# A fused encoder layer on one core: three instead of six low parts made by accumulating DMAs in the opening, and the first unit's products and one sum of h in another order

## The chip, the cores and the metric

The program runs on one core of a Trainium2 chip. The metric is the device time of one execution in microseconds (us); less is better. Before the change the median of three runs is 1087.13 us (1085.92 to 1087.98).

## What is computed

One encoder layer on a sequence of 512 tokens of width 1024, all in float32. A conditioning vector `c` gives nine modulation vectors (shift, scale and gate of three sublayers), then come a SwiGLU, two token mixers in parallel, and a second SwiGLU:

```
mod = silu(c) @ w_mod + b_mod                      # 1024 -> 9 x 1024
sh1, sc1, g1, sh2, sc2, g2, sh3, sc3, g3 = split(mod, 9)
h = rmsnorm(x, norm_ffn1) * (1 + sc1) + sh1
x = x + 0.5 * g1 * swiglu(h, w_ffn1_in, w_ffn1_out)      # inner width 2816
...                                                       # two attention mixers, gated
h = rmsnorm(x, norm_ffn2) * (1 + sc3) + sh3
x = x + 0.5 * g3 * swiglu(h, w_ffn2_in, w_ffn2_out)
```

Only the beginning matters here: the norm of `x`, `sc1` and `sh1`, `h`, and the first products with `w_ffn1_in`.

## The kernel before, in words

**High and low parts.** Every matrix product is made of three: each operand is split into a high part (rounded to a shorter format by a copy on ACT) and a low part (the rest), and high*high, high*low and low*high are summed in PSUM. A low part is made in one of two ways. Either DVE subtracts the high part from the raw tile (L607 in the opening, L786 in units, L170 in `split_from`), or ACT writes minus the raw tile, rounded, into the place of the low part (L600), and an accumulating DMA issued by POOL adds the matrix from HBM once more (L601).

**The opening** (`first_chunk`, L644 to L683) runs over k = 0 to 7, slices of 128 of the 1024 channels. For each k three transfers of 512 KB are queued on SP: the columns of `w_mod` for sc1 (called SC1 k here), the tile `w1s[k]` (raw k) and the columns for sh1 (SH1 k). DVE reduces each `w_mod` tile with silu(c) (L269), then L335 makes `x * scale * norm`, ACT adds the shift and rounds (L336: h high), and DVE makes the low part of h (L338). PE multiplies with L637: eight products of 512 columns with h high, eight with h low, and eight with the weights' low part, which from k = 1 on are put off (`rest1`) and come one or two chunks later. So PE needs 24 products for k = 0, 16 for k = 1 and 2, 24 for k = 3 to 6 and 40 for k = 7. The order on DVE is written out by hand: L335 of k, L269 for SC1 k+1, L338 of k, L269 for SH1 k+1, L607 of k+1 where there is one, and L335 of k+1.

`BY_DMA` (L115) lists the k whose low part is made by L600 and L601. The others have L607.

**The first unit** (`First`, L765 on) begins when the last L637 ends. A unit multiplies in Strassen's manner with seven products (24 matmuls of 256 columns each) instead of eight; their weights are the quarters a11, a12, a22 and the sums s1 = a21+a22, s2 = s1+a11, s3 = a11+a21, s4 = s2+a12, and their other operands the quarters of h and the sums n1, n2, t3, t4 (`h1_sum`, L750). s1, s3 and s4 come from accumulating DMAs of POOL (L778), s2 from DVE (L794). High parts of weights: L782 on ACT; low: L786 on DVE. Sums of h: L562 or L564 on DVE, L169 on ACT, L170 on DVE. Products of a11, s2, s3 and a22 share one PSUM bank (x), s1 and s4 another (v), a12 has a third (w). After a11, s1 and s2, ACT copies the bank out (L838), after s3 DVE adds it (L844), and the next product into that bank has to wait for it.

**The order of work.** All instructions of this stage stand in an order that the program computes from a list of steps with times (`steps1`) and tasks with due times (`tasks1`): a task is written down after the first step whose time is not smaller. `First.first` is the order of the products of the first unit, `times` in `First.tasks` holds the due times of the splits, and a tuple at L1009 those of the sums of h. The unit of `times` is one product, 2.72. Each engine then executes its instructions strictly in the order written.

Of the kernel before, what the change touches and what calls it, by code (L numbers as in the profile page):

```python
# [111 lines left out]

LAST = 2

BY_DMA = (1, 2, 3, 5, 6, 7)  # L115

TO_MIX = (4, 2, 2, 2, 4, 2, 1)
TO_FFN2 = (3, 1, 2, 2, 3, 2, 1)
# [6 lines left out]
def layer(ctx: ExitStack, tc: tile.TileContext, a: dict):  # L125
# [34 lines left out]
    def f(ap):  # L160
        return ap.bitcast(F32)
# [432 lines left out]
    def first_split(k):  # L594
# [3 lines left out]
        S.copy(hi, raw)  # L598
        if k in BY_DMA:
            S.activation(lo, raw, AF.Identity, scale=-1.0)  # L600
# [3 lines left out]
    def first_low(k):  # L604
        raw, hi, lo = w1[k][2:]
        if k not in BY_DMA:
            V.tensor_tensor(lo, raw, f(hi), ALU.subtract)  # L607
# [4 lines left out]
    n1 = Norm()  # L612
# [110 lines left out]
    n2 = Norm()  # L723
    act_h, act_l, act_t = [None] * NPAIR, [None] * NPAIR, {}

    def new_act(p):
        part = [r for r in ROUNDS if p in r][0]
        i = (p - part.start) // 4
        if (part.start, i) not in act_t:
            act_t[part.start, i] = b8(), b8()  # L730
            for q in range(part.start + 4 * i, min(part.start + 4 * i + 4, part.stop)):
                act_h[q], act_l[q] = (t[:, q - part.start - 4 * i, :] for t in act_t[part.start, i])
        return act_t[part.start, i], (p - part.start) % 4
# [16 lines left out]
    def h1_sum(t):  # L750

        p, q = SUMS[t]
        out = h1_at[q if t in ("t3", "t4") else p]
        if t == "t3":
            h1_op[t] = [u[:, :, HALVES[1]] for u in h1_tiles]
        else:
            o = b8()
            h1_op[t] = [o[:, :, r] for r in HALVES]
        for k in (slice(0, 2), slice(2, 4)):
            sub(out[:, k, :], h1_at[p][:, k, :], h1_at[q][:, k, :], t in NEGATED)  # L760
        for k in (slice(0, 2), slice(2, 4)):
            split_from(*(u[:, k, :] for u in h1_op[t]), out[:, k, :])
        h1_at[t] = out

    class First(Unit):  # L765

        order = ("a11", "s1", "s2", "a12", "s3", "s4", "a22")
        first = ("a11", "a12", "s1", "s2", "s3", "s4", "a22")

        def load(self, q):  # L770
            t = u4(F32).rearrange("p a b -> p (a b)") if q == "s1" else sbuf("raw", [P, 1024], F32, RAW)
# [26 lines left out]
        def tasks(self):  # L798
            early = self is units1[0]
            yield -6.7 if early else -13.0, lambda: self.load("s1")  # L800
            yield -5.3 if early else -11.0, lambda: self.add("s1", "s1", "a22")
            yield -6.5 if early else -9.5, lambda: self.load("a11")
            second = self is units1[1]
            yield -0.3 if early else -2.4 if second else -5.9, self.second
            yield -5.6 if early else -5.0, lambda: self.load("a12")
            yield -1.0, lambda: self.load("a22")
            times = dict(s1=-7, a11=-3, s2=-2, a12=-1, s3=2, s4=3, a22=3)
            if early:
                times.update(s1=-1.2, a11=-2.5, s2=-0.02, a12=-1.6, s4=3.05, a22=3.1)
            if second:  # L810
                times.update(s1=-3.5, s2=-1.5, a11=-4.2)
            for q, at in times.items():
                yield at, lambda q=q: self.high(q)
                yield at + (0.4 if early else 1.0), lambda q=q: self.low(q)
# [181 lines left out]
    def task1(at, do):  # L996
        heapq.heappush(tasks1, (at, task1.n, do))
        task1.n += 1
# [7 lines left out]
        task1(19.0 + 2.0 * q, lambda q=q: finish_high(q))  # L1006
        task1(21.0 + 2.0 * q, lambda q=q: finish_low(q))
    new_act(0)
    for t, at in (("n1", -16.0), ("n2", -5.0), ("t3", 2.6), ("t4", 11.0)):  # L1009
        task1(at, lambda t=t: h1_sum(t))  # L1010

    def multiply1(u, q, t0, last):
# [703 lines left out]
    with tc.manual_schedule(engines=BOUND):  # L1716
# [6 lines left out]
        at = TO_FFN2  # L1723
# [177 lines left out]
```

## Time and profile before

| | before |
|---|---|
| median of the runs | 1087.13 us (1085.92 to 1087.98) |
| the profiled execution, its own time | 1087.35 us |
| its span, first to last instruction | 1085.5 us |
| PE, DVE, ACT, POOL busy | 97%, 74%, 53%, 13% of the span |
| mean granted clock of PE | 0.997 |
| opening, from the first L637 to the first product of the first unit | 16.67 to 68.42 us |

The profile is one execution on the chip. A row of the timeline gives the start in us, the duration in us, engine, line, operation, tiles (written <- read), shapes and count, and in brackets how long the engine was idle before and who ended that. In the table by windows the columns are the length of the stretch, busy time and count of PE, PE's weight loads, DVE, ACT and POOL, the granted PE clock, the busy share of the DMA engines, and GB/s. The granted clock is told as a share of full speed. A duration on DVE or ACT can overlap the next one's start by some hundredths; the distance from start to start is what an instruction costs in a row of them.

### The profile page before, as it was taken

How to read it: one execution, taken by the hardware profiler on the slowest of the kernel's cores; microseconds unless marked ns; L12 is line 12 of the kernel's file. 1: busy time of each engine (PE TensorE's matmuls, PEld its weight loads, DVE VectorE, ACT ScalarE, POOL GpSimd, SP SyncE). 2: the span in 40 equal slices, each digit the busy share in tenths (PEclk: the TensorE clock that was granted, in tenths of full speed). 3: DMA queues.
4: the chain of work that ended last, by engine and by line, in shares of the span. 5: the costliest groups of instructions: out<-in, count | busy, mean ns of one | idle time of the engine just before them, and what ended most of it. 6: DMA issues, size and time to landing. Idle time of an engine off the chain costs nothing.

```text
span 1085.5 us, 18432 instructions
## 1 busy us (share of the span) xinstructions
PE 1057.8 (97%) x7228; PEld 952.8 (88%) x7228; DVE 800.8 (74%) x1446; ACT 574.0 (53%) x937; POOL 145.9 (13%) x165
## 2 busy tenths in 40 slices
PE   8799999999999999999999999999999999999998
PEld 6689889989998988866788877989999999999997
DVE  7768777687967845657853777995878776877877
ACT  6555335424653443666645556534765645654553
POOL 1110010001001100521002300001021111211210
PEclk9999999999999999999999999999999999999999
DMA  9995986788666394864358821885397999999974
GB/s 345 341 227 144 313 239 163 191 281 228 166 207 220 111 316 152 182 146 97 98 173 203 224 88 57 331 286 141 78 208 173 225 225 238 197 228 217 215 149 121
DMA packets 65193, 215.64 MB, mean 199 GB/s; under 512 B 7762, under 2 KB 9938, under 8 KB 65107
## 3 DMA queue, kind: packets, MB, share of 16 engines
q1 hardware_dynamic: 44496, 145.73, 38.9%
q0 software_dynamic: 18160, 64.50, 32.4%
q10 hardware_dynamic: 2450, 4.25, 1.0%
q8 instruction: 56, 0.92, 0.3%
q14 instruction: 31, 0.25, 0.1%
HBM read 205.53 MB, written 8.92 MB: 198 GB/s over the span
## 4 chain that ended last, share of the span: by engine, by line
PE 67%; issue 15%; DMA 8%; DVE 6%; POOL 2%; ACT 2%; ACTq 0%; SPq 0%; POOLq 0%; DVEq 0%
PE sc L164 6%; PE sc L166 6%; PE sc L165 5%; PE acc L434 3%; PE acc L435 3%; PE acc L436 3%; PE sc L436 3%; PE sc L434 3%; PE sc L435 3%; PE acc L164 3%; PE acc L165 3%; PE acc L166 3%; DMA u<-w2i 2%; PE acc L1132 2%; PE acc L1133 2%
## 5 line engine op out<-in xcount | busy, mean ns | idle before, releaser
L434 PE MATMUL acc<-b,high 128*128 128x256 f32 x614 | 170.9, 278 | 1.7 <-ACT f L838 0.7
L435 PE MATMUL acc<-b,high 128*128 128x256 f32 x614 | 170.5, 278 | 0.4 <-DVE b L170 0.3
L436 PE MATMUL acc<-b,low 128*128 128x256 f32 x614 | 170.3, 277 | 0.1
L169 ACT CAST high<-raw 128x1024 fp32r<-128x1024 f32 (+1 forms) x96 | 98.8, 1032 | 116.5 <-PE sc L1134 19.0
L170 DVE TENSOR_TENSOR low<-raw,high 128x1024 fp32r<-128x1024 f32 (+1 forms) x96 | 114.8, 1200 | 56.4 <-ACT high L169 56.2
L434 PE MATMUL sc<-b,high 128*128 128x256 f32 x550 | 152.3, 277 | 2.6 <-ACT f L502 2.6
L436 PE MATMUL sc<-b,low 128*128 128x256 f32 x550 | 152.3, 277 | 0.1
L435 PE MATMUL sc<-b,high 128*128 128x256 f32 x550 | 152.1, 277 | 0.0
L434 PEld LDWEIGHTS acc<-b,high 128*128 128x128 f32 x614 | 115.7, 188 | 2.8 <-ACT f L838 0.9
L435 PEld LDWEIGHTS acc<-b,high 128*128 128x128 f32 x614 | 115.8, 189 | 0.9 <-DVE b L170 0.5
L436 PEld LDWEIGHTS acc<-b,low 128*128 128x128 f32 x614 | 115.8, 189 | 0.3 <-DVE low L170 0.3
L434 PEld LDWEIGHTS sc<-b,high 128*128 128x128 f32 x550 | 103.3, 188 | 3.0 <-ACT f L502 3.0
L436 PEld LDWEIGHTS sc<-b,low 128*128 128x128 f32 x550 | 103.3, 188 | 0.5 <-DVE low L786 0.3
L435 PEld LDWEIGHTS sc<-b,high 128*128 128x128 f32 x550 | 103.3, 188 | 0.0
L165 PE MATMUL sc<-b,high 128*128 128x512 f32 (+1 forms) x272 | 99.1, 364 | 0.2 <-DVE b L170 0.2
L166 PE MATMUL sc<-b,low 128*128 128x512 f32 (+1 forms) x272 | 99.0, 364 | 0.3 <-DVE low L880 0.3
L164 PE MATMUL sc<-b,high 128*128 128x512 f32 (+1 forms) x272 | 99.0, 365 | 0.0
L164 PE MATMUL acc<-b,high 128*128 128x512 f32 (+1 forms) x200 | 74.6, 373 | 1.2 <-ACT b L169 0.6
L169 ACT CAST high<-u 128x1024 fp32r<-128x1024 f32 (+1 forms) x51 | 52.2, 1026 | 40.2 <-PE sc L435 9.3
L269 DVE CUSTOM_DVE_ANT_0 u<-u,ka,begin 128x1024 f32<-128x1024 f32 x48 | 62.6, 1310 | 13.9 <-DMA u<-w_mod 13.8
L170 DVE TENSOR_TENSOR low<-u,high 128x1024 fp32r<-128x1024 f32 (+1 forms) x51 | 60.7, 1191 | 15.0 <-ACT high L169 14.4
L165 PE MATMUL acc<-b,high 128*128 128x512 f32 (+1 forms) x200 | 71.7, 359 | 0.0
(382 smaller groups left out, 2711.4 us busy)
## 6 DMA issues: line engine op xcount, KB each, us to landing
u<-w_mod SPq DMA_DIRECT2D x66, 512.0 KB, 6.6
raw<-w2i SPq DMA_DIRECT2D x31, 512.0 KB, 5.1
u<-w2i POOLq DMA_DIRECT2D x31, 512.0 KB, 6.3
raw<-w1u SPq DMA_DIRECT2D x27, 512.0 KB, 5.3
u<-w1u POOLq DMA_DIRECT2D x18, 512.0 KB, 7.7
raw<-w1o SPq DMA_DIRECT2D x16, 512.0 KB, 4.4
raw<-w_gate SPq DMA_DIRECT2D x16, 512.0 KB, 4.1
low<-w_gate POOLq DMA_DIRECT2D x13, 512.0 KB, 7.4
```

The source lines that it names most:

```text
L164: PE.matmul(out, wh, xh, start=first, stop=False)
L165: PE.matmul(out, wh, xl, start=False, stop=False)
L166: PE.matmul(out, wl, xh, start=False, stop=last)
L169: S.copy(hi, src)
L170: V.tensor_tensor(lo, src, f(hi), ALU.subtract)
L269: summed = V.tensor_tensor_reduce(out=w, in0=w, in1=cact, scale=by, scalar=b, op0=ALU.mult, op1=ALU.add, accum_out=t,)
L434: PE.matmul(out, wh[:, s], xh, start=first and j == 0, stop=False, skip_group_check=True)
L435: PE.matmul(out, wh[:, s], xl, start=False, stop=False, skip_group_check=True)
L436: PE.matmul(out, wl[:, s], xh, start=False, stop=last and j == 1, skip_group_check=True)
L1132: PE.matmul(out[t][:, 0:n], hh[k][:, ht], wh[:, o : o + n], start=k == 0, stop=False)
L1133: PE.matmul(out[t][:, 0:n], hh[k][:, ht], wl[:, o : o + n], start=False, stop=False)
```

## The change

The low parts of k = 2, 3 and 6 are made by L607 on DVE, not by L600 and L601. In the first unit s2 is multiplied before s1. Of the due times, s4's split moves from 3.05 to 2.9 products, and the sum t4 from 11.0 to 8.0; s3 keeps its 2.

```diff
-BY_DMA = (1, 2, 3, 5, 6, 7)
+BY_DMA = (1, 5, 7)
...
         order = ("a11", "s1", "s2", "a12", "s3", "s4", "a22")
-        first = ("a11", "a12", "s1", "s2", "s3", "s4", "a22")
+        first = ("a11", "a12", "s2", "s1", "s3", "s4", "a22")
...
             if early:
-                times.update(s1=-1.2, a11=-2.5, s2=-0.02, a12=-1.6, s4=3.05, a22=3.1)
+                times.update(s1=-1.2, a11=-2.5, s2=-0.02, a12=-1.6, s3=2, s4=2.9, a22=3.1)
...
-    for t, at in (("n1", -16.0), ("n2", -5.0), ("t3", 2.6), ("t4", 11.0)):
+    for t, at in (("n1", -16.0), ("n2", -5.0), ("t3", 2.6), ("t4", 8.0)):
```

**DVE in the opening**, a piece of the difference between the two programs, around k = 2 and k = 3. raw_152 is raw 2 and raw_232 raw 3; x_80 and x_81 are the slices of x for k = 2 and 3.

```order
 L269 ISA u_29_154,mod_96<-u_29_154,ka_112,par 128x1024
 L269 ISA mod_96 128x1
+L607 TENSOR_TENSOR low<-raw_152,high 128x1024
 L335 SCALAR_TENSOR_TENSOR b_16_117<-x_80,mod_97,f_53_227 128x512
 L269 ISA u_55_230,mod_97<-u_55_230,ka_112,begin,par 128x1024
...
 L269 ISA u_57_234,mod_96<-u_57_234,ka_112,par 128x1024
 L269 ISA mod_96 128x1
+L607 TENSOR_TENSOR low<-raw_232,high 128x1024
 L335 SCALAR_TENSOR_TENSOR b_16_117<-x_81,mod_97,f_53_227 128x512
```

The subtract stands ahead of L335, which begins the making of h for the same k. A third one is added in the same place for k = 6; on ACT the three L600, and on POOL's queue three of the six L601, are gone. SP's queue has the same transfers in the same order.

**DVE in the first unit**, before. raw_442 is the tile of s3, u_70_440 that of s4, raw_573 that of a22, raw_534 that of the second unit's a11, acc_538 bank x, and the pair L562 and L170 is t4.

```order
L841 TENSOR_TENSOR f_83_587<-f_83_587,tp_589 128x512
L786 TENSOR_TENSOR low<-raw_442,high 128x1024
L786 TENSOR_TENSOR low<-u_70_440,high 128x1024
L786 TENSOR_TENSOR low<-raw_573,high 128x1024
L786 TENSOR_TENSOR low<-raw_534,high 128x1024
L844 TENSOR_TENSOR f_87_655<-f_87_655,acc_538 128x512
L562 SCALAR_TENSOR_TENSOR b_17_118<-b_16_117,b_17_118 128x2x256 x2
L170 TENSOR_TENSOR b_89_740<-b_17_118,b_89_740 128x2x256 x2
```

The same place with the change (the numbers in the names have moved: s3 is raw_439, s4 u_70_437, a22 raw_570, the second unit's a11 raw_531, bank x acc_535).

```order
L841 TENSOR_TENSOR f_83_584<-f_83_584,tp_586 128x512
L786 TENSOR_TENSOR low<-raw_439,high 128x1024
L562 SCALAR_TENSOR_TENSOR b_17_118<-b_16_117,b_17_118 128x2x256 x2
L170 TENSOR_TENSOR b_88_681<-b_17_118,b_88_681 128x2x256 x2
L786 TENSOR_TENSOR low<-u_70_437,high 128x1024
L786 TENSOR_TENSOR low<-raw_570,high 128x1024
L786 TENSOR_TENSOR low<-raw_531,high 128x1024
L844 TENSOR_TENSOR f_89_688<-f_89_688,acc_535 128x512
```

t4 now stands ahead of the low part of s4 and of L844, where it stood behind both.

**ACT at the same place**, with the change: copies of banks (L838), high parts (L782) and the high part of t4 (L169).

```order
L838 COPY f_86_651<-acc_535 128x512
L782 CAST high<-raw_531 128x1024
L782 CAST high<-u_70_437 128x1024
L169 CAST b_88_681<-b_17_118 128x2x256 x2
L838 COPY f_89_688<-acc_653 128x512
L782 CAST high<-raw_570 128x1024
```

The first L838 is that of s2 and the second that of s1; before, s1's copy came first, s2's followed the second unit's a11, and L169 of t4 stood behind the high parts of s4, a22 and the second unit's s1.

## The prediction

> **What bounds the kernel now.** I read the page first, then who waited for whom on PE in the part that the change touches, then the timeline there.
>
> ```profile
> span 1085.5 us, 18432 instructions
> PE 1057.8 (97%) x7228; PEld 952.8 (88%) x7228; DVE 800.8 (74%) x1446; ACT 574.0 (53%) x937; POOL 145.9 (13%) x165
> low<-w1s POOLq DMA_DIRECT2D x6, 512.0 KB, 8.7
> PE acc L637 <- ACT b L336: 6.6, 3, 4.6
> PE sc L434 <- ACT f L502: 2.6, 2, 1.4
> ```
>
> PE sets the time, so what counts is where it stands idle: 27.7 us in all. 6.6 us of it are waits of the opening's products for the high part of h, the longest 4.6; the last row is the longest of any later wait, 1.4. The timeline of PE shows where, and the pace when nothing is missing.
>
> ```profile
> 29.30 0.39 PE L637 MATMUL op<-b,high 128*128 128x512 f32 x1
> 30.92 0.50 PE L637 MATMUL acc<-b,high 128*128 128x512 f32 x1 [1.24 <-ACT b L336]
> 41.28 0.70 PE L637 MATMUL acc<-b,high 128*128 128x512 f32 x1 [4.62 <-ACT b L336]
> 48.48 0.39 PE L637 MATMUL acc<-b,high 128*128 128x512 f32 x1
> 53.91 0.39 PE L637 MATMUL acc<-b,high 128*128 128x512 f32 x1
> 68.42 0.28 PE L434 MATMUL acc<-b,high 128*128 128x256 f32 x1
> ```
>
> k = 3 starts at 30.92, k = 4 at 41.28, k = 5 at 48.48, k = 6 at 53.91, the first unit at 68.42. A chunk of 24 products at full pace takes 53.91 - 48.48 = 5.43 us, 0.226 each; k = 4 took 7.20, 1.77 more, because the clock was down after the pause of 4.62 us:
>
> ```profile
> 42.00:43.00 1.00, 1.00 (x3) 0.77 (x3) 1.00 (x2) 1.00 (x2) 0.00 (x0) 0.50 1.01 401
> 20.16 17.19 DMA u<-w_mod
> 20.00:23.50 3.50, 3.50 (x17) 2.91 (x16) 3.50 (x7) 2.67 (x4) 0.23 (x1) 1.00 1.03 405
> 31.50:35.50 4.00, 4.00 (x19) 3.32 (x18) 2.02 (x3) 0.00 (x0) 0.00 (x0) 1.00 1.05 281
> 35.50:37.50 2.00, 1.16 (x6) 0.62 (x4) 0.12 (x1) 1.67 (x2) 0.00 (x0) 1.00 1.03 420
> 19.32 0.92 POOL L601 DMA_DIRECT2D low<-w1s  x1 [5.51 <-ACT low L600]
> 23.75 0.88 POOL L601 DMA_DIRECT2D low<-w1s  x1 [3.52 <-ACT low L600]
> 27.55 0.86 POOL L601 DMA_DIRECT2D low<-w1s  x1 [2.92 <-ACT low L600]
> ```
>
> The second row is the chain's: behind the long pause stands one load, SH1 4, issued at 20.16 and landed at 37.35. In the windows the DMA engines are full throughout (share 1.03 to 1.05), but they move 405 to 420 GB/s before 23.5 us and after 35.5, and 281 between, while the accumulating DMAs of k = 1, 2 and 3 run. So the wait is for bandwidth.
>
> DVE between these loads:
>
> ```profile
> 23.85 0.75 DVE L335 SCALAR_TENSOR_TENSOR b<-x,mod,f 128x512 f32<-128x512 f32 x1
> 24.52 1.34 DVE L269 CUSTOM_DVE_ANT_0 u<-u,ka,begin 128x1024 f32<-128x1024 f32 x1
> 25.78 0.75 DVE L338 SCALAR_TENSOR_TENSOR b<-b,mod,b 128x512 fp32r<-128x512 f32 x1
> 28.16 1.28 DVE L269 CUSTOM_DVE_ANT_0 u<-u,ka,par 128x1024 f32<-128x1024 f32 x1 [1.63 <-DMA u<-w_mod]
> 37.38 1.28 DVE L269 CUSTOM_DVE_ANT_0 u<-u,ka,par 128x1024 f32<-128x1024 f32 x1 [3.37 <-DMA u<-w_mod]
> 38.59 1.22 DVE L607 TENSOR_TENSOR low<-raw,high 128x1024 fp32r<-128x1024 f32 x1
> 39.72 0.75 DVE L335 SCALAR_TENSOR_TENSOR b<-x,mod,f 128x512 f32<-128x512 f32 x1
> ```
>
> From start to start: L335 0.67, L269 for SC1 1.26, L338 about 0.67, L269 for SH1 1.21, L607 1.13. From L335's start to PE's first product of the same k it is 41.28 - 39.72 = 1.56 us.
>
> **The change, part by part.** *Accumulating DMAs.* From 23.5 to 35.5 us, 12 us, the engines moved 12 x 281 GB/s = 3.37 MB, of which 3 x 0.524 are the accumulations; the loads got 1.80 MB. At 420 GB/s they would have got 5.04. The difference, 3.24 MB, is 7.7 us of loading, 2.57 for each accumulating DMA. Two of the three, k = 2 and 3, ran before SH1 4 landed: it lands at 37.35 - 5.14 = 32.2. SH1 3, which DVE awaited until 28.16, comes hardly earlier, since k = 1's accumulation fills the time up to then; DVE gets there at 27.6, and I take 28.0.
>
> *Subtracts.* Each L607 costs 1.13 us in front of L335, on the path to h. k = 2: L335 at 23.85 + 1.13 = 24.98, PE at 26.54. PE is free at 29.53 - 16 x 0.226 = 25.91 (the last product of k = 2 before began at 29.30), so a new pause of 0.6. k = 2 ends at 26.54 + 0.1 (first product) + 3.62 = 30.26. k = 3: SH1 3 at 28.0, L607 29.21, L335 30.34, PE 31.90: a pause of 1.6, and 0.98 later than before. It ends at 31.90 + 0.1 + 5.43 = 37.43. k = 4: SC1 4 at 31.01 (its load, before SH1 4 in the queue, is there), L338 32.27, SH1 4 at 32.94 (landed 32.2, margin 0.7), L607 34.15, L335 35.28, PE could begin at 36.84; it is free at 37.43. No pause, and no reason for the clock to fall. For k = 5 DVE needs 3.8 us (the four without L607), for k = 6 with it 4.9, for k = 7 6.4 with n1 (2.6, as t4's rows below); PE needs 5.43 each time, so DVE, 0.6 ahead at k = 4, is 1.7 ahead at k = 7. So k = 5 starts at 42.86 and the first unit at 42.86 + (68.42 - 48.48) = 62.80: **5.6 us earlier**. The third subtract, k = 6, costs nothing under that cover; with the cover gone, 1.13. The three L600 saved cost nothing either: ACT waited for DVE before L336. POOL's queue loses three DMAs, so s1's accumulation moves up; it is needed before a product 5 us into the unit. SP now waits for a subtract before it reloads raw 2, 3 and 6, at places where the queue was waiting anyway.
>
> The new pauses need a price for the clock. The rows show 1.24 us of idling at 30.92 without a fall, and 4.62 with one. 1.6 is near the first, so I put the fall at zero, with 1.77 as the other end. The Trainium skill, "TensorE: Matmul & The Clock Gate", section Part 1, lets the clock fall only after an idle window of about 3.4 us; by that the sum is the same as by the nearer row, and both rows agree with it.
>
> *First unit.* PE, then DVE, ACT and POOL before:
>
> ```profile
> 80.26 0.38 PE L434 MATMUL acc<-b,high 128*128 128x256 f32 x1 [0.68 <-ACT f L838]
> 86.59 0.38 PE L434 MATMUL acc<-b,high 128*128 128x256 f32 x1 [0.61 <-ACT b L169]
> 87.31 0.38 PE L435 MATMUL acc<-b,high 128*128 128x256 f32 x1 [0.34 <-DVE b L170]
> 76.68 1.22 DVE L786 TENSOR_TENSOR low<-raw,high 128x1024 fp32r<-128x1024 f32 x1
> 84.60 0.68 DVE L844 TENSOR_TENSOR f<-f,acc 128x512 f32<-128x512 f32 x1
> 85.20 1.29 DVE L562 SCALAR_TENSOR_TENSOR b<-b,b 128x512 f32<-128x512 f32 x2
> 86.57 1.29 DVE L170 TENSOR_TENSOR b<-b,b 128x512 fp32r<-128x512 f32 x2
> 87.78 1.22 DVE L786 TENSOR_TENSOR low<-u,high 128x1024 fp32r<-128x1024 f32 x1
> 77.39 1.05 ACT L782 CAST high<-raw 128x1024 fp32r<-128x1024 f32 x1
> 80.10 1.05 ACT L782 CAST high<-u 128x1024 fp32r<-128x1024 f32 x1
> 85.92 1.22 ACT L169 CAST b<-b 128x512 fp32r<-128x512 f32 x2 [2.87 <-DVE b L562]
> 71.48 0.86 POOL L778 DMA_DIRECT2D u<-w1u  x1 [1.38 <-DMA u<-w_mod]
> DMA to landing us min/median/max: 5.7/6.6/9.9
> ```
>
> s3 at 80.26 waited for the copy of s2 out of the same bank, a22 at 86.59 and 87.31 for t4. A product takes about 2.72 us (six of them 16.4 with the first one's 0.1), so without waits the seven would end 19.1 after the unit's start T; with 87.31 as the second matmul of the last, they ended near 90.04, T + 21.6. With s1 between s2 and s3, s2's copy has a product's time: that wait goes.
>
> What is late next is DVE, which works without a break. Its row of s3's low part at T + 8.26 (76.68) frees it at T + 9.4. Then t4: L562. ACT has s2's copy, the second unit's a11 at T + 9.0 (77.39), s4's high part at T + 9.9 if its DMA is there, and t4's L169 from T + 10.9; L170 begins 0.65 later, at T + 11.55, and frees DVE 1.21 later, at T + 12.8. s4's low part is done at T + 13.9, and PE asks for it at T + 13.95: no wait, or 0.1. Then two more L786 to T + 16.1 and L844, 0.6 from 84.60 to 85.20, to T + 16.8; a22 needs its bank, and would be ready at T + 16.4: it waits 0.4 and ends at T + 19.55. **2.05 us saved** (2.45 without that wait). s4's DMA is issued at T + 3.1 (71.48) behind s2's low part; with the median of 6.6 us it lands at T + 9.7, in time.
>
> *Sum.* The second unit's order is the same and hangs on PE; from there to the end no wait of PE is above the 1.4 us of the first rows, and I move it all unchanged. 5.6 + 2.05 = 7.65. The profiled execution took 1087.35 us, 1.85 more than its span, 0.2 above the median of the runs: 1087.35 - 7.65 = **1079.7 us**. By itself it has 1078 to 1081: SH1 3 at 27.6 gives 0.4, L844 in time 0.4, and single runs lie 1.0 about their median.
>
> **The rivals.**
> - *The clock falls in the pause of 1.6 us*: +1.77, 1081.5. For it: two pauses close together; against: the row of 1.24.
> - *An accumulation costs the loads only its own bytes*, 0.524 MB at 420 GB/s, 1.25 us. SH1 4 lands at 34.85, k = 4 starts at 38.74, +1.3: 1081.0. Against it: 281 GB/s. The Trainium skill, "DMA: Bandwidth & Descriptors", section Anatomy of one DMA — SWDGE (gpsimd) path, fits such a DMA by 2.0 us plus its bytes at 436 GB/s, an estimate of 1.2 us of data here; the 8.7 us of the rows above do not fit it.
> - *s4 lands late.* Since t4's L169 stands behind s4's high part on ACT, a landing at L puts the end of a22 at L + 9.6. With 9.9 us, the longest of these DMAs, that is T + 22.6: 1082.8.
> - *The opening gains nothing*: the freed bandwidth goes to later loads, SH1 4 lands at 37.35 still, and only the unit's 2.05 is left: 1085.3, within 0.2%.
> - *Slower*: the same queue behind s4, but its DMA takes as long as SH1 4's load, 17.19 us, since the loads of the units now meet it. It decides from 16.8 us on (L = 82.6); with 17.19 a22 ends at 92.6 instead of 90.04: 1089.9. Against it: those 17 us had eight loads ahead of it, and at T the queue has few.
> That the change would not do what it says is no case: the rows of the two programs show it.
>
> **How the numbers follow.** The forecast has 0.66, the clock 0.09, cheap accumulations 0.08, s4 late 0.08, no gain in the opening 0.06, slower 0.03. The first four are faster by over 0.2% (about what a measurement of this kernel tells from no change): 0.91; within: 0.06; slower: 0.03. The range takes the first four with the spread of runs, 1077.5 to 1083.2, and leaves out 0.09 and the tails.
>
> **What would show it.** PE's first product of k = 2, 3, 4 near 26.5, 31.9 and 37.4 us, clock at 1.00 throughout; about 420 GB/s from 28 us on; SH1 4 not awaited; first unit at 62.8; no wait of s3 for L838, a short one of a22 for L844. Wrong: DVE still awaits SH1 4 past 33.6, a clock of 0.50, or PE awaits s4's low part by over a microsecond.

## The result and the profile after

The changed kernel takes 1081.21 us (median of 5 runs, 1079.6 to 1082.83) against 1087.13 (1085.92 to 1088.22, 5 runs). The ratio is 0.9946, with a 95% interval of 0.9931 to 0.9961: 5.9 us faster, between 4.2 and 7.5. The forecast of 1079.7 us, a ratio of 0.9932, lies near the fast end of that interval. The profiled execution took 1080.83 us, 6.5 less than that of before.

The page of the changed kernel, its span and the busy time of each engine:

```profile
span 1079.1 us, 18430 instructions
PE 1055.2 (98%) x7228; PEld 951.4 (88%) x7228; DVE 803.8 (74%) x1449; ACT 571.1 (53%) x934; POOL 143.3 (13%) x162
```

PE has the same 7228 instructions and stands idle for 23.9 us instead of 27.7. Its busy time fell too, by 2.6 us, though its work is the same: part of that is the spell at half clock, which counted as busy. DVE has three instructions more, ACT three fewer, POOL three fewer. Whom PE waited for from 14 to 112 us (sum, count, longest):

```profile
PE acc L637 <- ACT b L336: 2.3, 3, 1.0
PE acc L434 <- DVE f L844: 0.2, 1, 0.2
```

The opening's waits are down from 6.6 us to 2.3, and no wait for L838, L169 or L170 is left in the first unit. PE's timeline, the first products of k = 2, 3 and 4, of the first unit, of a22's second half and of the second unit:

```profile
26.40 0.50 PE L637 MATMUL acc<-b,high 128*128 128x512 f32 x1 [0.50 <-ACT b L336]
31.34 0.50 PE L637 MATMUL acc<-b,high 128*128 128x512 f32 x1 [1.01 <-ACT b L336]
36.92 0.39 PE L637 MATMUL acc<-b,high 128*128 128x512 f32 x1
62.31 0.28 PE L434 MATMUL acc<-b,high 128*128 128x256 f32 x1
79.27 0.36 PE L434 MATMUL acc<-b,high 128*128 128x256 f32 x1 [0.18 <-DVE f L844]
82.08 0.28 PE L434 MATMUL sc<-b,high 128*128 128x256 f32 x1
```

The pause of 4.62 us before k = 4 is gone, and the first unit begins at 62.31 instead of 68.42. The windows say why (columns: length, busy time and count of PE, PEld, DVE, ACT and POOL, granted clock, DMA share, GB/s):

```profile
20.00:23.50 3.50, 3.50 (x18) 2.88 (x17) 3.50 (x5) 2.39 (x3) 0.09 (x1) 1.00 1.06 401
23.50:27.50 4.00, 3.50 (x16) 2.59 (x15) 4.00 (x8) 1.67 (x2) 0.00 (x0) 1.00 1.02 282
27.50:31.50 4.00, 2.99 (x14) 2.17 (x13) 4.00 (x6) 1.67 (x3) 0.00 (x0) 1.00 1.02 417
31.50:35.50 4.00, 4.00 (x18) 3.29 (x19) 4.00 (x8) 1.46 (x3) 0.00 (x0) 1.00 1.03 418
38.00:42.00 4.00, 4.00 (x19) 3.30 (x19) 4.00 (x7) 3.12 (x5) 0.87 (x1) 1.00 1.03 410
42.00:46.00 4.00, 4.00 (x20) 3.30 (x19) 4.00 (x7) 1.78 (x3) 0.00 (x0) 1.00 1.07 293
```

The low rate now lasts 4 us, not 12, the clock is 1.00 in each window, and from 23.5 us DVE works without a break where before it stood still for up to 3.37 us. SP issued SH1 4 at the same time as before, 20.02 here (the first of the two) against 20.16:

```profile
20.02 2.26 SPq L234 DMA_DIRECT2D u<-w_mod  x2
```

So the load is not asked for earlier; it arrives earlier. In the opening DVE does not wait for loads any more, and PE now waits for DVE. DVE's timeline around k = 2 and 3, the L269 for SH1 4, then around t4 in the first unit:

```profile
23.71 1.22 DVE L607 TENSOR_TENSOR low<-raw,high 128x1024 fp32r<-128x1024 f32 x1
24.85 0.74 DVE L335 SCALAR_TENSOR_TENSOR b<-x,mod,f 128x512 f32<-128x512 f32 x1
27.44 1.28 DVE L269 CUSTOM_DVE_ANT_0 u<-u,ka,par 128x1024 f32<-128x1024 f32 x1
28.64 1.22 DVE L607 TENSOR_TENSOR low<-raw,high 128x1024 fp32r<-128x1024 f32 x1
29.78 0.74 DVE L335 SCALAR_TENSOR_TENSOR b<-x,mod,f 128x512 f32<-128x512 f32 x1
32.37 1.28 DVE L269 CUSTOM_DVE_ANT_0 u<-u,ka,par 128x1024 f32<-128x1024 f32 x1
...
73.82 1.29 DVE L170 TENSOR_TENSOR b<-b,b 128x512 fp32r<-128x512 f32 x2 [0.84 <-ACT b L169]
75.03 1.22 DVE L786 TENSOR_TENSOR low<-u,high 128x1024 fp32r<-128x1024 f32 x1
78.44 0.68 DVE L844 TENSOR_TENSOR f<-f,acc 128x512 f32<-128x512 f32 x1
```

Both subtracts stand right ahead of an L335, SH1 4 is there when DVE comes to it at 32.37, and L844 comes after the low parts. The time can be split at three points on PE's timeline: the opening from the first L637 (16.53 us) to the first unit, the first unit up to the second, and the rest up to the start of the last matmul.

| kernel | opening, us | first unit, us | rest, us |
|---|---|---|---|
| before | 51.75 | 21.63 | 990.68 |
| changed | 45.78 | 19.77 | 992.52 |

The opening gives 5.97 us and the unit 1.86, 7.83 in all. The rest of this execution is 1.84 us longer.

### The profile page after: what moved, and what is told of

Its sections match the earlier page's. It is cut to its first block, busy times and chain, and to the rows that moved or that the text cites. A ratio compares the mean times of both kernels' runs of the same rounds, so it can differ in the third digit from the quotient of the medians.

```text
span 1079.1 us, 18430 instructions
## 1 busy us (share of the span) xinstructions
PE 1055.2 (98%) x7228; PEld 951.4 (88%) x7228; DVE 803.8 (74%) x1449; ACT 571.1 (53%) x934; POOL 143.3 (13%) x162
## 4 chain that ended last, share of the span: by engine, by line
PE 68%; issue 13%; DMA 8%; DVE 7%; ACT 2%; POOL 2%; SPq 0%; ACTq 0%; DVEq 0%; POOLq 0%
PE sc L164 6%; PE sc L166 6%; PE sc L165 5%; DMA u<-w2i 4%; PE acc L434 4%; PE acc L435 4%; PE acc L436 4%; PE sc L436 3%; PE sc L434 3%; PE sc L435 3%; PE acc L164 3%; PE acc L165 3%; PE acc L166 3%; PE acc L1132 2%; PE acc L1134 2%
## 5 line engine op out<-in xcount | busy, mean ns | idle before, releaser
L169 ACT CAST high<-raw 128x1024 fp32r<-128x1024 f32 (+1 forms) x96 | 98.8, 1032 | 120.7 <-PE sc L1134 19.1
L170 DVE TENSOR_TENSOR low<-raw,high 128x1024 fp32r<-128x1024 f32 (+1 forms) x96 | 114.7, 1198 | 56.6 <-ACT high L169 56.4
L169 ACT CAST high<-u 128x1024 fp32r<-128x1024 f32 (+1 forms) x51 | 52.3, 1025 | 41.2 <-PE sc L435 6.7
L269 DVE CUSTOM_DVE_ANT_0 u<-u,ka,begin 128x1024 f32<-128x1024 f32 x48 | 62.5, 1308 | 12.9 <-DMA u<-w_mod 12.8
L166 PE MATMUL acc<-b,low 128*128 128x512 f32 (+1 forms) x200 | 71.3, 356 | 0.0
```

What stands on the lines that cost most here:

```text
L166: PE.matmul(out, wl, xh, start=False, stop=last)
L169: S.copy(hi, src)
L170: V.tensor_tensor(lo, src, f(hi), ALU.subtract)
L269: summed = V.tensor_tensor_reduce(out=w, in0=w, in1=cact, scale=by, scalar=b, op0=ALU.mult, op1=ALU.add, accum_out=t,)
```

## The experiments

**The theory** is the prediction's: an accumulating DMA takes 2.57 us of loading from the loads queued beside it, so with three of them SH1 4 comes about 5 us sooner, the long pause and the fall of the clock behind it go, and the subtracts come back only as two short pauses. In the unit, the two moves each take away one wait. **The rivals**: that an accumulation costs the loads only its own bytes; that it is the place of the work on DVE, not the traffic, that moves the opening; and that in the unit one of the two moves does all.

Ratios are each against the kernel before, run beside it on the same chip. The stages are those of the table above.

### The two parts apart

Only the three accumulating DMAs, on the kernel before:

```diff
-BY_DMA = (1, 2, 3, 5, 6, 7)
+BY_DMA = (1, 5, 7)
```

> Only the three low parts of k = 2, 3 and 6 go from accumulating DMAs to DVE; the first unit is as before. Theory (bandwidth): the opening shortens as in the whole change, k = 3 starts on PE near 31.3 us, k = 4 near 36.9, the clock stays at 1.00, the first unit starts near 62.4; the unit keeps its waits, 0.7 for the copy of s2 and about 1 for t4, so the second unit is 6.1 us earlier than before, and the time is 1081 if all of it reaches the end. Rival (the two parts lean on each other): without the new order the waits in the unit grow, since PE comes to it earlier than its data, and the time is above 1083. Second question: if the end is less than 6.1 us earlier while the second unit is, something after it gives time back.

Measured: 1082.92 us (before 1088.7), ratio 0.9954 (0.9937 to 0.9971). The opening takes 46.21 us, the unit 21.63. PE's timeline, the first product of k = 3 and the unit's two waits:

```profile
31.81 0.50 PE L637 MATMUL acc<-b,high 128*128 128x512 f32 x1 [1.47 <-ACT b L336]
74.61 0.38 PE L434 MATMUL acc<-b,high 128*128 128x256 f32 x1 [0.68 <-ACT f L838]
80.94 0.38 PE L434 MATMUL acc<-b,high 128*128 128x256 f32 x1 [0.61 <-ACT b L169]
```

Of the opening's 5.97 us, 5.54 are there. The difference is SH1 3, for which DVE waited until 27.91 in this execution, where in the change it was there at 27.44:

```profile
27.91 1.28 DVE L269 CUSTOM_DVE_ANT_0 u<-u,ka,par 128x1024 f32<-128x1024 f32 x1 [0.36 <-DMA u<-w_mod]
```

The unit has its old length to 0.01 us with its old waits, 0.68 and 0.61, only 5.65 us earlier.

Only the order of the unit, on the changed kernel:

```diff
-BY_DMA = (1, 5, 7)
+BY_DMA = (1, 2, 3, 5, 6, 7)
```

> Only the first unit's order (s2 before s1) and the due times of s4 and t4; all six accumulating DMAs stay. Theory (two separate gains): the opening ends at 68.4 us as before, the wait for the copy of s2 is gone and that for t4 becomes a wait of 0.2 to 0.4 for the add after s3; the second unit starts 1.9 us earlier, 1085.2. Rival: in the opening that is full of traffic s4's accumulation lands late, ACT stands before t4, and PE waits for s4's low part over a microsecond: 1086.5 or more.

Measured: 1085.93 us, ratio 0.9975 (0.9962 to 0.9989). The unit takes 19.87 us, the opening 49.56. PE's timeline, k = 4 and a22, and a window behind the pause:

```profile
39.98 0.80 PE L637 MATMUL acc<-b,high 128*128 128x512 f32 x1 [4.05 <-ACT b L336]
84.00 0.36 PE L434 MATMUL acc<-b,high 128*128 128x256 f32 x1 [0.18 <-DVE f L844]
41.00:42.00 1.00, 1.00 (x4) 0.80 (x3) 1.00 (x2) 1.00 (x2) 0.00 (x0) 0.50 1.00 410
```

The pause before k = 4 is back (4.05 us) and with it the low clock (0.50), while the unit keeps its 1.8 us. The two parts do not touch each other. The opening is 2.2 us shorter than before the change with the same instructions in it, which was not expected: SH1 4 landed sooner in this execution, as the last section shows.

### What the opening hangs on: traffic, or the place of the work

The traffic back, with the subtracts left in their new places as work whose result is not used (a third edit, not shown, lets a later pair of tiles use the memory of `idle`):

```diff
-BY_DMA = (1, 5, 7)
+BY_DMA = (1, 2, 3, 5, 6, 7)
...
+    idle = keep([P, 1024], "idle")
...
+        elif k in (2, 3, 6):
+            V.tensor_tensor(idle, raw, f(hi), ALU.subtract)
```

> The whole change on DVE with the DMAs of before: L600 and L601 stay for all six k, and the three subtracts are made as well, at their new places, into a tile that nobody reads. Theory (bandwidth): the loads are as slow as before, DVE awaits SH1 4 until about 37.4 us, PE starts k = 4 at 41.3 or later with the clock at 0.50 behind the pause, the first unit starts at 68.4 or up to 1 us later, and the time is 1085 to 1086. Rival (the gain is from POOL's and ACT's lighter queues or from the places of the subtracts, not from bytes): DVE does not wait for SH1 4, first unit near 62.5, 1081.

Measured: 1086.62 us, ratio 0.9986 (0.9972 to 1.0). The opening takes 49.27 us against 45.78, the unit 20.57, with a wait of 0.68 for the low part of s4. DVE's timeline, the L269 for SH1 4 and for SH1 7, and PE's, the first products of k = 4 and k = 7 (L640 here is L637 elsewhere):

```profile
35.45 1.28 DVE L269 CUSTOM_DVE_ANT_0 u<-u,ka,par 128x1024 f32<-128x1024 f32 x1 [2.06 <-DMA u<-w_mod]
52.18 1.28 DVE L269 CUSTOM_DVE_ANT_0 u<-u,ka,par 128x1024 f32<-128x1024 f32 x1 [2.46 <-DMA u<-w_mod]
39.35 0.50 PE L640 MATMUL acc<-b,high 128*128 128x512 f32 x1 [1.34 <-ACT b L336]
57.53 0.50 PE L640 MATMUL acc<-b,high 128*128 128x512 f32 x1 [1.55 <-ACT b L336]
```

One window of it:

```profile
28.00:32.00 4.00, 3.26 (x15) 2.35 (x13) 4.00 (x6) 2.30 (x4) 0.86 (x1) 1.00 1.06 297
```

With the same work on DVE, the three accumulations, with their L600 on ACT, bring the rate down to 297 GB/s and DVE's waits back, and what DVE waits for are loads, not ACT. So the place of the work on DVE does not explain the gain; the traffic does. The expected size was missed, though: k = 4 began at 39.35, where the theory had 41.3, and the first unit at 66.74 instead of 68.4 or later. SH1 4 came 1.4 to 1.9 us sooner than in the profiles of before, and neither of the two pauses shown lowered the clock.

The other way round, the same three DMAs, and the subtracts of k = 2, 3, 4 and 6 left out. ACT's L600 runs in their place, so these four low parts stay incomplete and the result is not the layer's:

```diff
-        if k in BY_DMA:
+        if k:
             S.activation(lo, raw, AF.Identity, scale=-1.0)
+        if k in BY_DMA:
...
-        if k not in BY_DMA:
+        if k == 0:
```

> The whole change without the subtracts of k = 2, 3, 4 and 6: in their low parts stands minus the raw tile as ACT's L600 writes it, so those low parts are wrong and DVE has 1.13 us less a chunk, ACT 0.95 more. Theory (the pauses left are subtracts ahead of L335): no pause at k = 2; at k = 3 DVE now waits for SH1 3 until about 27.4 us and PE for at most 0.8 us; opening 44.2 to 45.0 us. Rival (the loads hold h up again as soon as DVE is faster): pauses of 1.5 us or more remain, opening 45.5 to 45.8 us.

Measured, one execution: 1076.57 us (before 1087.7). The opening takes 44.16 us. DVE's timeline, the L269 for SH1 3 and SH1 4:

```profile
27.24 1.28 DVE L269 CUSTOM_DVE_ANT_0 u<-u,ka,par 128x1024 f32<-128x1024 f32 x1 [0.58 <-DMA u<-w_mod]
31.97 1.28 DVE L269 CUSTOM_DVE_ANT_0 u<-u,ka,par 128x1024 f32<-128x1024 f32 x1 [0.55 <-DMA u<-w_mod]
```

Here DVE, without the subtracts, reaches the loads first and shows when they land: SH1 4 at 31.97, where the sum had 32.2 and the rival of cheap accumulations 34.85. The four subtracts, that of k = 4 from before the change among them, cost 45.78 - 44.16 = 1.6 us of the opening. The whole kernel's gain over the change, about 4 us in single executions, is more than that, and the rest of it lies in the last 990 us, which this edit does not touch: it is part of the spread discussed below.

### The subtract in a later place

The subtract of k behind the making of h for k, instead of ahead of it:

```diff
-            first_low(k + 1)
...
             if k == 0:
                 mod_col(SC1, 1, w1[1][0])
+        else:
+            first_low(k)
```

> The whole change, with the subtract of k put after the low part of h of the same k instead of ahead of L335 of k. Theory (the two new pauses of 0.5 and 1.0 us at k = 2 and 3 come from subtracts ahead of L335): the pause at k = 2 is gone, that at k = 3 falls to about 0.7 since the subtract of k = 2 is still ahead of L335 of k = 3; first unit at 61.6, 0.8 us below the whole change. Rival (h waits for its loads): the pauses stay, first unit at 62.4, no difference.

Measured: 1080.22 us, ratio 0.9928 (0.9909 to 0.9948); opening 44.62 us. PE's timeline, k = 3:

```profile
30.77 0.50 PE L637 MATMUL acc<-b,high 128*128 128x512 f32 x1 [0.67 <-ACT b L336]
```

The pause at k = 2 is gone and that at k = 3 is down from 1.01 to 0.67, and the opening gains 1.16 us over the change. That is more than the 0.84 us of idle time, because the time in brackets falls short of a pause's cost: from k = 1's first product to k = 2's it is 3.62 us here and 4.29 in the change, 0.67 for a pause of 0.50. The kernel beats the kernel before clearly; against the change the intervals overlap.

A step later again, the subtract of k - 1 behind the making of h for k:

```diff
-            first_low(k + 1)
...
+        if k > 1:
+            first_low(k - 1)
...
-        wh, wl = w1.pop(k)[3:]
+        wh, wl = w1[k][3:]
```

> The whole change, with the subtract of k put behind L335 of k + 1, so that no subtract of the opening but the first stands ahead of L335 of k = 2 and 3. Theory (the pauses left are DVE's time in front of L335): the pause at k = 2 is gone, that at k = 3 is 0 if SH1 3 has landed by 26.5 us, and up to 0.8 if only by 27.4; first unit after 44.1 to 44.9 us from the first L637, against 45.8 with the change and 44.6 with the subtract behind the low part of h. Rival (raw tiles are given back later now, and SP's queue stands behind that): DVE awaits loads for k = 6 or 7, opening 45.8 us or longer.

Measured: 1080.52 us, ratio 0.9927 (0.9914 to 0.9941); opening 45.64 us, no better than the change. DVE's timeline, the L269 for SH1 3:

```profile
29.50 1.28 DVE L269 CUSTOM_DVE_ANT_0 u<-u,ka,par 128x1024 f32<-128x1024 f32 x1 [2.01 <-DMA u<-w_mod]
```

PE's timeline, k = 3:

```profile
32.27 0.50 PE L637 MATMUL acc<-b,high 128*128 128x512 f32 x1 [1.65 <-ACT b L336]
```

The theory made the pause hang on SH1 3, but had it land by 27.4 at the latest. It landed at 29.50 in this execution, 2 us after DVE was ready for it, and PE paused for 1.65 us; it was the only pause behind the first product. Of the 2.1 us beyond 27.4, 1.1 are a late start of the whole execution (first L637 at 17.63, against 16.53 in the change); the rest is the load's. What the later place saved on DVE was lost to a load. The clock stayed at 1.00 through this pause.

### The two moves in the unit

Both kernels have the three DMAs and the unit of before, with one move each. The swap of s1 and s2 alone:

```diff
-        first = ("a11", "a12", "s1", "s2", "s3", "s4", "a22")
+        first = ("a11", "a12", "s2", "s1", "s3", "s4", "a22")
```

> Three accumulating DMAs as in the change, and s2 before s1, but the due times of s4 and t4 as before the change. Theory (the last product's wait for t4 is set by DVE's order, not by PE's): the wait of s3 for the copy of s2 goes, but t4 is still written behind s4's and two more subtracts and the add after s3, so the last product starts at almost the same distance from the unit's start: unit 21.4 us against 21.6 before and 19.8 with both. Rival (the two waits are independent and each goes with its own edit): 20.8 us.

Measured: 1084.4 us (before 1088.4), ratio 0.9965 (0.9951 to 0.9979). The unit takes 21.62 us, as before the change. PE's timeline, the first product of a22 and the next:

```profile
80.50 0.39 PE L434 MATMUL acc<-b,high 128*128 128x256 f32 x1 [1.33 <-ACT b L169]
81.22 0.39 PE L435 MATMUL acc<-b,high 128*128 128x256 f32 x1 [0.34 <-DVE b L170]
```

The wait of s3 for s2's copy is gone, and the wait for t4 grew by as much, from 0.61 to 1.33: t4's time is set by DVE and ACT, so PE came sooner and waited longer.

t4's earlier due time alone:

```diff
-    for t, at in (("n1", -16.0), ("n2", -5.0), ("t3", 2.6), ("t4", 11.0)):
+    for t, at in (("n1", -16.0), ("n2", -5.0), ("t3", 2.6), ("t4", 8.0)):
```

> Three accumulating DMAs as in the change, t4 written at 8.0 products, but s1 before s2 and s4's split as before. Theory (DVE's order sets the end of the unit): s3 still waits 0.7 for the copy of s2, then t4 is ready and the last product follows s4 without a wait: unit 20.1 us. Rival (independent waits): the same order of size, 20.2; so this run tells whether the two edits add up, together with the run of the swap alone: by the theory 0.2 and 1.5 us, by the rival 0.85 and 1.4 with a sum above the 1.9 of both.

Measured: 1081.55 us, ratio 0.9942 (0.9922 to 0.9962). The unit takes 20.16 us. PE's timeline, s3, the only wait left:

```profile
73.98 0.39 PE L434 MATMUL acc<-b,high 128*128 128x256 f32 x1 [0.71 <-ACT f L838]
```

The swap alone saves 0.0 us, t4 alone 1.5, the whole change 1.86. The second wait stood behind the first, so the swap pays only once t4 is out of the way. The earlier split of s4 (3.05 to 2.9), which the change also has, was not run by itself.

### How much comes back by itself

The changed kernel once more, and the kernel before twice more, for its opening in other executions.

> The changed kernel once more, to tell the size of its gain and to see where what PE has gained by the second unit goes. PE's stages up to there as before: opening 45.8 us from the first L637 to the first unit, unit 19.8 us. Theory (the loss behind is scatter of the late stages): from the second unit to the end between 989.5 and 992.7 us, and a gain of 7 to 8 us in the medians. Rival (the gain is in part given back in the second SwiGLU because PE comes earlier): 992.5 or more again, and a gain near 6 us.

> The kernel before, profiled again: how much of its long pause at k = 4 is in every execution? Theory (bandwidth, so any shift of the transfers moves it): opening between 49.5 and 52 us from the first L637 to the first unit, unit 21.6 us, the wait for SH1 4 between 3 and 5 us, and from the second unit to the end 989.5 to 992. Rival (a fixed order of transfers): opening 51.7 and the rest 990.7 again, within 0.2 us.

> The same a second time, with the same expectations: opening 49.5 to 52 us by the theory, 51.7 by the rival; unit 21.6 us; the rest 989.5 to 992 by the theory of scatter, and 990.7 if it is fixed.

Measured: the change 1081.55 us, ratio 0.9939 (0.9925 to 0.9953), with 45.76, 19.86 and 993.24 us for the opening, the unit and the rest. The kernel before, one execution each, 1088.11 and 1088.53 us, with 52.10 and 51.67 us for the opening, 21.63 and 21.61 for the unit, 991.23 and 991.91 for the rest. PE's timeline of the second of these, k = 4:

```profile
40.73 0.79 PE L637 MATMUL acc<-b,high 128*128 128x512 f32 x1 [5.51 <-ACT b L336]
```

The long pause of before is no accident of one execution, though its length is not fixed: the opening of 52.10 lies 0.1 us above the range that was expected, and neither the openings nor the rests repeat within the 0.2 us of the rival. By the mean of three profiles of before (73.46 us for the opening and the unit) and two of the change (65.58), the change has gained 7.88 us when the second unit begins. Of the change's second profile, the rest of 993.24 us lies above the range of the scatter theory (989.5 to 992.7) and where the rival had it, that the gain is in part given back because PE comes earlier; the gain of 6.9 us in the medians lies between the two.

## Why the prediction was right, and where its steps were off

**The bandwidth step held.** In the changed kernel the one accumulation issued near 20 us leaves one window at 282 GB/s: of 4 x 282 = 1.13 MB, 0.52 are its own, and the loads get 0.60 where 4 us at 420 would give 1.68. The loss, 1.08 MB at 420 GB/s, is 2.6 us; the prediction had 2.57. The window from 42 us, with k = 5's accumulation, gives 2.5 in the same way. SH1 4 landed at 31.97 where nothing hid it, and e5_traffic brought the waits back with the three DMAs and their L600. The Trainium skill, "DMA: Bandwidth & Descriptors", section Anatomy of one DMA — SWDGE (gpsimd) path, fits a DMA of this path by 2.0 us plus its bytes at 436 GB/s, from which the prediction's estimate of 1.2 us of data came; here the measured price to the other loads is twice that.

**The new pauses** were 0.50 us at k = 2 (predicted 0.6) and 1.01 at k = 3 (predicted 1.6), at k = 4 none. The term that was mis-sized is SH1 3's landing: I took 28.0, but DVE began its L269 at 27.44 with no wait, as early as it could come. It is a matter of the execution, for in e1_dma_only, whose opening has the same instructions, SH1 3 was awaited until 27.91 and k = 3 began at 31.81 (predicted 31.90) after a pause of 1.47. With 27.44, k = 4 began at 36.92 instead of 37.43 and the first unit at 62.31 instead of 62.80. DVE then was ahead, as the sum had it, and the third subtract, at k = 6, cost nothing: no PE wait is left for k = 4 to 7. The whole cost of the four subtracts of the opening, 1.6 us, is what e4_no_subtract showed.

**The clock stayed** at 1.00, which settles that rival here, and the saving of 1.77 us for the slow chunk came in full: the pauses are 0.50 + 1.01 where they were 1.24 + 4.62, which is 4.35 us less, and 4.35 + 1.77 = 6.1 is near the 5.97 that the opening gave. The Trainium skill, "TensorE: Matmul & The Clock Gate", section Part 1, puts the fall behind an idle window of about 3.4 us; the runs agree, with pauses of 1.01, 1.34 and 1.65 us that lowered nothing, and 4.05 and more that did.

**The unit** saved 1.86 us, not 2.05. DVE's chain came as predicted: L170 of t4 at T + 11.51 (predicted 11.55), s4's low part at T + 12.72 (12.8), L844 at T + 16.13 (16.1), with T = 62.31. The wait of a22 for its bank was 0.18 instead of 0.4, but the six products ahead of it took 16.78 us where I had 16.4, so the unit ended at T + 19.77 instead of T + 19.55. s4 came in time. Where I had the two moves as two waits that go, e6_swap_only showed that the swap by itself saves nothing: the sum was right only because both were made.

**"From there to the end I move it all unchanged"** is the step that failed, if any: 7.88 us were gained at the second unit, and 5.9 and 6.9 in the two medians. Part of the difference may lie in the 7.88: e2_order_only, with the same instructions in its opening as before, took 49.56 us for it. With it as a fourth, the opening of before takes 51.27 us in the mean, against 45.87 in the five profiles with the change's opening, and the gain at the second unit is 7.2. The trace of the change has waits of PE past 760 us that the rows of before did not have, all in the second SwiGLU. From 752 to 792 us in the change:

```profile
PE tp L434 <- ACT high L169: 1.7, 1, 1.7
```

and from 1044 to 1079:

```profile
PE sc L436 <- DVE low L170: 0.5, 1, 0.5
PE acc L434 <- DVE f L504: 0.3, 1, 0.3
PE sc L434 <- ACT high L169: 0.3, 1, 0.3
```

In the changed kernel's second profile, from 752 to 835:

```profile
PE sc L434 <- ACT f L502: 2.8, 1, 2.8
PE tp L434 <- ACT high L169: 1.7, 1, 1.7
```

Before, from 760 to 800, had the second of these with less:

```profile
PE tp L434 <- ACT high L169: 0.7, 1, 0.7
```

So the limit of 1.4 us for later waits, which I read from one execution, does not hold for every one, of the kernel before either: its two further profiles have later waits of 2.1 and 1.8 us. Whether the change causes the new waits is not settled, but the other runs narrow it down. From 750 to 860 us the wait for L169 is 1.4 to 1.8 us in nine of the ten profiles in which PE comes to the second unit earlier than before, and 0.6 to 0.8 in the three of before (in the tenth, e3_low_later, it is 0.7, but the wait for L502 there is 2.9). The nine include e2_order_only, with its six accumulating DMAs:

```profile
PE tp L434 <- ACT high L169: 1.7, 1, 1.7
```

So this microsecond of idle time goes with PE's earlier arrival, whichever edit brings it. The time does not follow that wait alone: e7_t4_only has it too (1.7 us) and a rest of 990.22, and the rest is 991.5 us in the mean of the ten and 991.3 in that of the three. The stretch from the second unit to about 760 us is equal in all profiles, within 2 us; the whole rest took 989.5 to 991.9 us in five profiles with six accumulating DMAs (mean 990.9) and 989.4 to 993.2 in eight with three (mean 991.8). The difference of 0.8 us has a standard error of 0.6, from spreads of 0.9 and 1.4. No run moves the second SwiGLU's transfers without moving its start, so it stays open whether some 0.8 us of the gain is given back there or the profiles only fell so.

**The version that is better still.** e3_low_later takes the pause at k = 2 away and has the shortest opening of the kernels that compute everything, 44.62 us, 1.16 less than the change. Its median of 1080.22 and that of e8_low_next, 1080.52, are the lowest, and both beat the kernel before clearly. That either beats the change is likely from the stages for e3_low_later, though from one profile, and not shown by the intervals. Counted from the start of the span its first unit comes only 0.58 us sooner (61.73 against 62.31), since its first L637 came that much later.

## What to carry to other kernels

When loads wait and the DMA engines are full, divide the rate into who moves the bytes: a transfer that lowers the rate of all others costs more than its bytes, and moving its work to an engine with idle time can pay, even if that engine stands on the path, as long as the new pauses stay short. Where two waits lie one behind the other in a unit, removing the first alone moves it into the second, so cost both together. And a gain worked out for the first tenth of a program is only as sure as the rest is still: take the spread of the rest from several profiles before promising tenths of a per cent.

## What the runs showed of the hardware that was not expected

The accumulating DMA acts late: issued on POOL at 19.17 us, it leaves the rate at 401 GB/s until 23.5 and lowers it to 282 for the next 4 us (in windows of 1 us, 311 from 23 to 24, 266 to 279 up to 27, and 402 from 27 to 28). The same comes again with the one issued at 38.42: POOL's timeline,

```profile
19.17 0.92 POOL L601 DMA_DIRECT2D low<-w1s  x1 [5.51 <-ACT low L600]
38.42 0.87 POOL L601 DMA_DIRECT2D low<-w1s  x1 [18.33 <-ACT low L600]
```

and the windows above have 410 GB/s from 38 to 42 us, then 293.

Loads in the same queue order come up to 2 us apart in different executions. SH1 4 was awaited until 37.38, 37.17 and 36.83 us in three profiles of before and until 36.08 in e2_order_only, which has the same instructions in the opening. Counted from its issue that is 17.2, 17.2, 16.6 and 15.1 us. The opening took 51.67 to 52.10 us in the three and 49.56 in the fourth, a difference of over a third of what the change gains there.

Pauses of PE of 1.34 us (e5_traffic) and 1.65 us (e8_low_next) in the opening left the clock at 1.00, while those of 4.05, 4.62 and 5.51 us each also brought a spell at half clock: k = 4 then took 7.12, 7.20 and 7.71 us instead of 5.43, so 1.7 to 2.3 us more. The time at half clock is not fixed by the pause either: another pause of 4.62 us, in the first of the two further profiles of before, was followed by a k = 4 of 7.62 us.
